# Weight-stationary matmuls of a hybrid encoder: the high and low parts of the tokens as one moving stream of 512 columns

## The chip, the cores and the metric

The kernel runs on one core of one Trainium2 chip. The metric is the device time of one execution in microseconds; for the kernel before it is the median of three runs.

## What is computed

The reference is an encoder of two layers over 256 positions of width 1024, in fp32. Each layer has three sub-layers behind an RMSNorm:

```python
for l in range(DEPTH):
    h = rmsnorm(x, mix_norm_g[l])
    x = x + hybrid_mixer(h, ...)      # h @ w_in, then attention, SSD and Fourier branches, gated and projected
    h = rmsnorm(x, xattn_norm_g[l])
    m = rmsnorm(mem, mem_norm_g[l])
    x = x + memory_cross_attention(h, m, ...)
    h = rmsnorm(x, ffn_norm_g[l])
    x = x + (silu(h @ w_gate) * (h @ w_up)) @ w_down
```

The SSD branch takes the columns x, B and C of `h @ w_in` (3072 columns) through a depthwise convolution of 7 taps along the positions, and then SiLU. The FFN is 2816 wide.

## The kernel before

Every large product is made of three fp32r matmuls: both factors are split into a part `hi` (rounded to fp32r) and a rest `lo`, and hi·hi + hi·lo + lo·hi is accumulated in PSUM. The weights arrive as a stream of 125 pieces per layer, 1 MB each (`PLAN`). `load_next` (L310) issues a piece's DMA on SyncE, `split_next` (L321) makes `wh` on ScalarE (L327) and `wl` on VectorE (L328). `done` (L342) splits the piece three after the one just used (NHL = 3 buffers of each kind), so a piece's `wl` is written while the pieces ahead of it are used.

Two helpers use the pieces. `lin` (L362) keeps tokens stationary and moves 512 weight columns per matmul (L357 to L359). `lina` (L401) keeps 128 weight columns stationary and moves the 256 tokens, so that its result stands transposed, channels on partitions; it serves the 12 pieces per layer of B, C and x (`xbc_pieces`, L1091) and 18 pieces of FFN gate and up (L1426). A `lina` piece is 8 contraction tiles by 256 columns; its two blocks of 128 columns share one PSUM bank, and each block runs, per contraction tile:

```python
T.matmul(o, hi[:, w0:w0 + P], sh[:, k, :], start=kt == 0, stop=False)
T.matmul(o, hi[:, w0:w0 + P], sl[:, k, :], start=False, stop=False)
T.matmul(o, lo[:, w0:w0 + P], sh[:, k, :], start=False, stop=kt == npk - 1)
```

The accumulators rotate over four banks (`acc`, L235); four others (`tp`) serve transposes and small products. When a piece of x, B or C is done, `conv_pair` (L696) copies the bank to SBUF on ScalarE (L699) and leaves the convolution (12 VectorE instructions, L710, and what is around them) as a background task. In the FFN `gate_f` applies SiLU straight from the bank (L1415) and `up_f` multiplies straight from the bank (L1419) before it splits the result for the down projection (L1422, L1423).

All other work (convolution, SSD, attention, Fourier, norms) is written as generators in seven lanes. `pump` (L281) runs them, piece by piece, against a budget of VectorE microseconds; a task that yields SOON or LATER is held back for some pumps (NWAIT = 1 for the norm lane, WAIT = 4). SBUF scratch comes in slots of 4 KB (23) and 2 KB (13) per partition: a foreground request that finds four or fewer free ones runs background steps until more are free (`slot`, L198, RESERVE = 4), and a background task waits until the slots that it declares are there. Within an engine the compiler's scheduler then orders the instructions, except on TensorE inside `ordered()`.

Below, piece n is the n-th of a layer, from 0; pieces 6 to 9 are B and C, 10 and 11, 24 and 25, 30 and 31, 38 and 39 are x, 14 to 17 gate columns, 95 and up the FFN's.

Of the kernel before, what the change touches and what calls it, by code (L numbers as in the profile page):

```python
# [31 lines left out]
NRAW, NHL = 3, 3  # L32
NS4, NS2 = 23, 13
LATER, SOON = "later", "soon"
LANES = ("n", "s", "c", "a", "t0", "t1", "f")
WAIT = 4
XWAIT = 3
NWAIT = 1
CAP = 6.0
# [136 lines left out]
def trunk(ctx: ExitStack, tc: tile.TileContext, a, out):  # L176
# [12 lines left out]
    def nm(p):  # L189
# [4 lines left out]
    slots = {4: deque(sp.ring(4096, name=f"r4_{i}") for i in range(NS4)),  # L194
             2: deque(sp.ring(2048, name=f"r2_{i}") for i in range(NS2))}
    owner = {}

    def slot(size, shape, dt):  # L198
        keep = 0 if running[0] else RESERVE
        while len(slots[size]) <= keep and step():  # L200
            pass
        if not slots[size]:
            raise RuntimeError(f"no slot of {size} KB")
        r = slots[size].popleft()
        t = r.tile(shape, dt, name=nm("s%d_" % size))
        owner[id(t)] = (size, r, t)
        return t
# [154 lines left out]
    def lin(act, npieces, on_done, nk=8, seg=None, us=BUDGET, par=False, before=None, mid=None):  # L362
# [5 lines left out]
        for si, n in enumerate(segs):  # L368
# [3 lines left out]
            for tt in range(2):  # L372
                if tt and not si and mid:
                    mid()
                for i, (w, k0, npk, n0, n_), (hi, lo) in ps:
                    if first is None:
                        first = n0
                    for c0 in range(0, n_, 512):
                        for kk in range(npk):
# [5 lines left out]
                            kt = k0 + kk  # L385
                            sh, sl = act(kt)
                            k = cnt[tt, ch]
# [13 lines left out]
    def lina(act, npieces, on_done, us=BUDGET):  # L401

        for _ in range(npieces):
            i, (w, k0, npk, n0, n_), (hi, lo) = take()
            us_ = us * npk * n_ / 2048
            for c0 in range(0, n_, 256):
                if c0:
                    pump(us_ / 2)
                nb = min(2, (n_ - c0) // P)
                ps = acc()  # L410
                with ordered():
                    for b in range(nb):
                        for kt in range(npk):
                            sh, sl = act(kt)
                            w0 = kt * n_ + c0 + b * P
                            o = ps[:, b * S:(b + 1) * S]
                            k = kt % 4
                            T.matmul(o, hi[:, w0:w0 + P], sh[:, k, :], start=kt == 0, stop=False)  # L418
                            T.matmul(o, hi[:, w0:w0 + P], sl[:, k, :], start=False, stop=False)  # L419
                            T.matmul(o, lo[:, w0:w0 + P], sh[:, k, :], start=False, stop=kt == npk - 1)  # L420
                on_done(n0 + c0, ps[:, :nb * S].rearrange("p (a b) -> p a b", a=nb))
            if n_ <= 256:
                pump(us_ / 2)
            done(i, us_)

# [60 lines left out]
    def put_f(pt, hl, tt, scale=None, n=4, par=False):  # L486

        hi, lo = hl
        pv = pt[:, :n * P].rearrange("p (a b) -> p a b", a=n)
        o = slice(tt, S, 2) if par else slice(tt * P, tt * P + P)  # L490
        if scale is None:
            A.copy(hi[:, :n, o], pv)  # L492
            V.tensor_sub(lo[:, :n, o], pv, hi[:, :n, o].bitcast(F32))  # L493
        else:
            A.activation(hi[:, :n, o], pv, AF.Copy, scale=scale)
            V.scalar_tensor_tensor(lo[:, :n, o], pv, scale, hi[:, :n, o].bitcast(F32),
                                   op0=ALU.mult, op1=ALU.subtract)

    def ftiles(n):
# [9 lines left out]
    nc.sync.dma_start(rb[32:35, :], a["c_sel"])  # L509
    h = ftiles(2)  # L510
    load_next()
# [184 lines left out]
    def conv_pair(ps, blk, cw, fin):  # L696

        u = s2([P, 2, S])
        A.copy(u, ps)  # L699

        def work():
# [3 lines left out]
            for b in range(2):  # L705
# [6 lines left out]
                yield 2.0  # L712
            free(u)
            A.activation(t, v, AF.Tanh, scale=0.5)
# [297 lines left out]
    for l in range(L):  # L1012
# [55 lines left out]
        def dt_columns():  # L1068
# [5 lines left out]
            for kt in range(8):  # L1074
                sh, sl = hb(kt)
# [41 lines left out]
        for n, tok in enumerate(ORDER):  # L1117
# [46 lines left out]
        free(h)  # L1164
        drain()
# [27 lines left out]
        gbx = bcast(a["xattn_norm_g"][l:l + 1, :], D)  # L1193
        hx = ftiles(2)

# [163 lines left out]
        lin(fl(hx), 4, query, seg=[1, 1, 1, 1])  # L1359
        free(hx)  # L1360
        vx.extend((s4([P, 2, 512], F32R), s4([P, 2, 512], F32R)) for _ in range(2))
# [19 lines left out]
        gbf = bcast(a["ffn_norm_g"][l:l + 1, :], D)  # L1381
        hf = ftiles(2)
        lin(fl(ox), 4, residual(gbf, hf), seg=[1, 3], before=drain)
# [42 lines left out]
        for c in range(9):  # L1426
            lina(fb, 1, gate_f)
            lina(fb, 1, up_f)
        free(hf)
        if l + 1 < L:  # L1430
            gbn = bcast(a["mix_norm_g"][l + 1:l + 2, :], D)
            h = ftiles(2)
            fin = residual(gbn, h)
# [46 lines left out]
```

## Time and profile before

| | |
|---|---|
| median of 3 runs | 1614.32 us (1613.74 to 1614.4) |
| the profiled execution | 1612.18 us, of it span 1610.1 us |
| TensorE matmuls | 8994, busy 99% of the span |
| VectorE busy | 1163.8 us (72%) |
| ScalarE busy | 956.5 us (59%) |
| GpSimd busy | 43.8 us (3%) |
| granted TensorE clock | 1.000 |

Busy matmul rows overlap, since a matmul starts before its predecessor's modelled end. So the cost of a matmul is read as the distance from one start to the next, and a wait of TensorE as idle time in front of an instruction.

### The profile page before, as it was taken

The page shows a single profiled execution, that of the slowest core. Times are in us where ns is not written, and L with a number is a line of the kernel's source. Part 1 is how long each engine was busy: PE and PEld are TensorE (multiplying, and loading weights), DVE is VectorE, ACT ScalarE, POOL GpSimd, SP SyncE. Part 2 cuts the span into 40 slices and gives each one's busy share as a digit, 9 for nine tenths or more (in the row PEclk, how much of TensorE's full clock was granted, in tenths as well). Part 3 has the DMA queues.
Part 4 walks back from the last instruction along what each step waited for, and adds up shares of the span by engine and source line. Part 5 has one row for each costly group of instructions (what it writes and reads, how often), then busy time and mean ns, then how long its engine had stood idle before and what let it go on. Part 6 is the DMA issues. An engine that isn't in the chain of part 4 may idle for free.

```text
span 1610.1 us, 22777 instructions
## 1 busy us (share of the span) xinstructions
PE 1592.1 (99%) x8994; PEld 1381.0 (86%) x8994; DVE 1163.8 (72%) x1777; ACT 956.5 (59%) x1587; POOL 43.8 (3%) x47
## 2 busy tenths in 40 slices
PE   8999999999999999999999999999999999999999
PEld 6998888888887888999889888888888878889997
DVE  5999997889757566555478999978886576565543
ACT  5666868787445664444356678677964457554442
POOL 0000000000000100000000000000100001000000
PEclk9999999999999999999999999999999999999999
DMA  8446655455556444555554577455555545345552
GB/s 298 159 161 230 223 182 181 167 196 192 196 196 223 177 153 162 198 183 184 183 190 146 182 230 242 154 189 179 172 185 203 202 181 196 131 169 175 183 190 95
DMA packets 84579, 299.46 MB, mean 186 GB/s; under 512 B 7305, under 2 KB 46857, under 8 KB 52728
## 3 DMA queue, kind: packets, MB, share of 16 engines
q1 hardware_dynamic: 84472, 298.01, 52.8%
q8 instruction: 70, 1.15, 0.3%
q14 instruction: 37, 0.30, 0.1%
HBM read 296.77 MB, written 1.22 MB: 185 GB/s over the span
## 4 chain that ended last, share of the span: by engine, by line
PE 91%; DVE 4%; ACT 2%; DMA 1%; POOL 1%; issue 1%; SPq 0%; DVEq 0%; ACTq 0%; POOLq 0%
PE acc L358 20%; PE acc L357 20%; PE acc L359 20%; PE acc L418 7%; PE acc L419 7%; PE acc L420 7%; PE tp L869 1%; PE tp L477 1%; PE tp L357 1%; PE tp L359 1%; PE tp L358 1%; PE tp L619 1%; DVE wl L328 1%; PE tp L940 1%; ACT wh L327 1%; PE tp L870 1%
## 5 line engine op out<-in xcount | busy, mean ns | idle before, releaser
L328 DVE TENSOR_TENSOR wl<-wr,wh 128x2048 fp32r<-128x2048 f32 (+1 forms) x256 | 572.6, 2239 | 278.5 <-ACT wh L327 277.9
L327 ACT CAST wh<-wr 128x2048 fp32r<-128x2048 f32 (+1 forms) x256 | 477.6, 1867 | 387.8 <-PE acc L359 184.3
L357 PE MATMUL acc<-wh,s 128*128 128x512 f32 x1520 | 604.4, 398 | 0.1
L358 PE MATMUL acc<-wl,s 128*128 128x512 f32 x1520 | 599.6, 395 | 1.6 <-DVE wl L328 1.6
L359 PE MATMUL acc<-wh,s 128*128 128x512 f32 x1520 | 596.2, 393 | 0.0
L358 PEld LDWEIGHTS acc<-wl,s 128*128 128x128 f32 x1520 | 288.0, 189 | 61.7 <-DVE wl L328 3.9
L357 PEld LDWEIGHTS acc<-wh,s 128*128 128x128 f32 x1520 | 287.9, 189 | 59.3 <-issue 1.4
L359 PEld LDWEIGHTS acc<-wh,s 128*128 128x128 f32 x1520 | 287.8, 189 | 58.0 <-issue 0.4
L418 PE MATMUL acc<-s,wh 128*128 128x256 f32 x960 | 273.3, 285 | 0.0
L419 PE MATMUL acc<-s,wh 128*128 128x256 f32 x960 | 271.7, 283 | 0.0
L420 PE MATMUL acc<-s,wl 128*128 128x256 f32 x960 | 271.6, 283 | 0.0
L418 PEld LDWEIGHTS acc<-s,wh 128*128 128x128 f32 x960 | 184.1, 192 | 1.1 <-issue 0.7
L419 PEld LDWEIGHTS acc<-s,wh 128*128 128x128 f32 x960 | 184.2, 192 | 0.8 <-issue 0.5
L420 PEld LDWEIGHTS acc<-s,wl 128*128 128x128 f32 x960 | 184.1, 192 | 0.0
L710 DVE SCALAR_TENSOR_TENSOR s<-s,cw,s 128x254 f32<-128x254 f32 (+2 forms) x288 | 120.9, 476 | 0.3
L841 ACT ACTIVATE s<-s,nacs 128x128 f32<-128x128 f32 x128 | 46.4, 392 | 13.4 <-DVE s L852 5.6
L844 ACT ACTIVATE s<-s,dt 128x128 f32<-128x128 f32 x128 | 45.3, 394 | 0.0
L842 DVE SCALAR_TENSOR_TENSOR s<-s,nacs,s 128x128 f32<-128x128 f32 x128 | 42.4, 344 | 3.5 <-ACT s L841 3.5
L845 DVE SCALAR_TENSOR_TENSOR s<-s,dt,s 128x128 f32<-128x128 f32 x128 | 41.5, 343 | 0.0
L493 DVE TENSOR_TENSOR s<-tp,s 128x512 fp32r<-128x512 f32 x56 | 36.9, 683 | 5.3 <-ACT s L492 5.2
L1199 DVE TENSOR_TENSOR X<-X,acc 128x512 f32<-128x512 f32 x24 | 16.4, 684 | 27.9 <-PE acc L359 27.9
L461 ACT ACTIVATE s<-X 128x512 f32<-128x512 f32 x24 | 15.1, 630 | 35.6 <-DVE X L1199 33.4
(224 smaller groups left out, 1418.8 us busy)
## 6 DMA issues: line engine op xcount, KB each, us to landing
wr<-in_wstream SPq DMA_DIRECT2D x248, 1024.0 KB, 4.8
s<-dd SPq DMA_DIRECT2D x32, 512.0 KB, 5.1
s<-in_wstream SPq DMA_DIRECT2D x6, 512.0 KB, 3.3
s<-vd SPq DMA_DIRECT2D x12, 256.0 KB, 5.9
wr<-in_wstream SPq DMA_DIRECT2D x8, 256.0 KB, 5.3
s<-in_ssd_norm_g SPq DMA_DIRECT2D x8, 256.0 KB, 3.2
s<-in_memT SPq DMA_DIRECT2D x4, 512.0 KB, 6.4
X<-in_x SPq DMA_DIRECT2D x2, 512.0 KB, 3.6
```

Source lines behind the costliest of these rows:

```text
L327: A.copy(hi[:, c], raw[:, c])
L328: V.tensor_sub(lo[:, c], raw[:, c], hi[:, c].bitcast(F32))
L357: T.matmul(o, sh, mh, start=start, stop=False)
L358: T.matmul(o, sh, ml, start=False, stop=False)
L359: T.matmul(o, sl, mh, start=False, stop=stop)
L418: T.matmul(o, hi[:, w0:w0 + P], sh[:, k, :], start=kt == 0, stop=False)
L419: T.matmul(o, hi[:, w0:w0 + P], sl[:, k, :], start=False, stop=False)
L420: T.matmul(o, lo[:, w0:w0 + P], sh[:, k, :], start=False, stop=kt == npk - 1)
L710: V.scalar_tensor_tensor(v[:, b, i0:i1], u[:, b, i0 + k - 3:i1 + k - 3], c[:, k:k + 1], v[:, b, i0:i1], op0=ALU.mult, op1=ALU.add)
L841: A.activation(E[:, j, :], b[:, 1, :], AF.Identity, bias=nacs[:, tt, 32 + hf:33 + hf])
L842: V.scalar_tensor_tensor(E[:, j, :], b[:, 0, :], nacs[:, tt, hf:hf + 1], E[:, j, :], op0=ALU.add, op1=ALU.min)
L844: A.activation(W[:, j, :], cbd[:, tt, 0, :], AF.Copy, scale=dt[:, tt, hf:hf + 1])
```

## The change

`lina` gives each block of 128 columns a PSUM bank of its own. The stationary `hi` weights are loaded once per contraction tile, and the tokens' `hi` and `lo` move as one stream of 2 x 256 columns, so that hi·hi lands in one half of the bank and hi·lo in the other. The `lo` weights still move the tokens' `hi` alone, into the first half. The two halves are added afterwards: on GpSimd after two copies in `conv_pair`, on VectorE from PSUM in the FFN (`halves`). For the two-part stream a norm's output (`h`, `hx`, `hf`) now has `hi` and `lo` in one tile, from two new 8 KB slots per pair, and the 4 KB slots fall from 23 to 19. NWAIT goes from 1 to 2, which holds back the transposes of a norm for one pump more.

```diff
-NS4, NS2 = 23, 13
+NS4, NS2, NS8 = 19, 13, 2
-NWAIT = 1
+NWAIT = 2
     def slot(size, shape, dt):
-        keep = 0 if running[0] else RESERVE
+        keep = 0 if running[0] or size == 8 else RESERVE
...
     def lina(act, npieces, on_done, us=BUDGET):
+            ps = []
+            for b in range(n_ // P):
+                ps.append(acc().rearrange("p (a b) -> p a b", a=2))
                 with ordered():
+                    for kt in range(npk):
+                        sh, _, hl = act(kt)
+                        k, w0, last = kt % 4, kt * n_ + b * P, kt == npk - 1
+                        small = lambda: T.matmul(ps[b][:, 0, :], lo[:, w0:w0 + P], sh[:, k, :], start=False, stop=False)
+                        if last:
+                            small()
+                        T.matmul(ps[b], hi[:, w0:w0 + P], hl[:, :, k, :], start=kt == 0, stop=last)
+                        if not last:
+                            small()
+            on_done(n0, ps)
...
+    def inputs_f():
+        ts = [slot(8, [P, 2, 4, S], F32R) for _ in range(2)]
+        return [(t[:, 0], t[:, 1], t) for t in ts]
...
     def conv_pair(ps, blk, cw, fin):
-        u = s2([P, 2, S])
-        A.copy(u, ps)
+        uu = s4([P, 2, 2, S])
+        for b in range(2):
+            A.copy(uu[:, b], ps[b])
+        u = uu[:, :, 0, :]
+        G.tensor_tensor(u, u, uu[:, :, 1, :], op=ALU.add)
...
+        def halves(t, ps):
+            for b in range(2):
+                A.copy(t[:, b], ps[b][:, 1, :])
+                V.tensor_add(t[:, b], t[:, b], ps[b][:, 0, :])
         def gate_f(n0, ps):
-            gs[n0] = s2([P, 2, S])
-            A.activation(gs[n0], ps, AF.Silu)
+            t = gs[n0] = s2([P, 2, S])
+            halves(t, ps)
+            A.activation(t, t, AF.Silu)
         def up_f(n0, ps):
-            t = gs[n0]
-            V.tensor_mul(t, t, ps)
+            t, r = gs[n0], s2([P, 2, S])
+            halves(r, ps)
+            V.tensor_mul(t, t, r)
```

The order of TensorE in an FFN gate piece, before (`s_618`, `s_619` are the tokens' `hi` and `lo`, `acc_117` the bank):

```order
L418 MATMUL acc_117<-s_618_5455,wh_5759 128x256
L419 MATMUL acc_117<-s_619_5456,wh_5759 128x256
L420 MATMUL acc_117<-s_618_5455,wl_5760 128x256
L418 MATMUL acc_117<-s_618_5455,wh_5759 128x256
L419 MATMUL acc_117<-s_619_5456,wh_5759 128x256
```

and in the changed kernel, at the end of a block and the start of the next (`s_614`, `s_615` hold both parts of the first and the last four contraction tiles):

```order
L419 MATMUL acc_114<-s_615_5318,wh_5969 128x512
L416 MATMUL acc_114<-s_615_5318,wl_5970 128x256 x2
L419 MATMUL acc_114<-s_615_5318,wh_5969 128x512
L419 MATMUL acc_115<-s_614_5317,wh_5969 128x512
L416 MATMUL acc_115<-s_614_5317,wl_5970 128x256
```

Two matmuls of 512 and 256 columns stand where three of 256 stood, and the next block goes to another bank.

The order of VectorE in the mixer of the first layer, between the `wl` of piece 16 and that of piece 17, before (L710 is the convolution, L786 the split of a finished pair of B or C):

```order
L328 TENSOR_TENSOR wl_1212<-wr_1033,wh_1211 128x2048
L786 TENSOR_TENSOR s_80_584<-s_145_1167,s_79_583 128x512
L710 SCALAR_TENSOR_TENSOR s_159_1287<-s_118_935,cw_209,s_159_1287 128x254
L710 SCALAR_TENSOR_TENSOR s_168_1372<-s_127_1020,cw_209,s_168_1372 128x254
L710 SCALAR_TENSOR_TENSOR s_159_1287<-s_118_935,cw_209,s_159_1287 128x253
L710 SCALAR_TENSOR_TENSOR s_168_1372<-s_127_1020,cw_209,s_168_1372 128x255
L710 SCALAR_TENSOR_TENSOR s_168_1372<-s_127_1020,cw_209,s_168_1372 128x253
L328 TENSOR_TENSOR wl_1246<-wr_1132,wh_1245 128x2048
```

and in the changed kernel the last ten rows ahead of the same `wl` (lines 12 higher there: L722 was L710, L826 was L814, the masking of C·B, L329 was L328):

```order
L722 SCALAR_TENSOR_TENSOR s_157_1243<-s_137_1065,cw_205,s_157_1243 128x255
L826 SCALAR_TENSOR_TENSOR s_159_1261<-tp_110,tri 128x128
L722 SCALAR_TENSOR_TENSOR s_157_1243<-s_137_1065,cw_205,s_157_1243 128x255
L826 SCALAR_TENSOR_TENSOR s_159_1261<-tp_110,tri 128x128
L722 SCALAR_TENSOR_TENSOR s_157_1243<-s_137_1065,cw_205,s_157_1243 128x254
L826 SCALAR_TENSOR_TENSOR s_159_1261<-tp_110,tri 128x128
L722 SCALAR_TENSOR_TENSOR s_157_1243<-s_137_1065,cw_205,s_157_1243 128x253
L826 SCALAR_TENSOR_TENSOR s_159_1261<-tp_110,tri 128x128
L722 SCALAR_TENSOR_TENSOR s_157_1243<-s_137_1065,cw_205,s_157_1243 128x253
L329 TENSOR_TENSOR wl_1305<-wr_1073,wh_1304 128x2048
```

Between the two `wl` stand 6 instructions before and 42 in the changed kernel: 22 of L722, 16 of L826, 2 of L727 and 2 of L798. On TensorE the 24 small matmuls of C·B (L357 to L359 into `tp`), which stood at pieces 17 and 18, now stand at pieces 14 to 16.

## Rows read from the trace of the kernel before

**Rows 1.** The page: busy time, VectorE in 40 slices, chain that ended last.
```profile
PE 1592.1 (99%) x8994; PEld 1381.0 (86%) x8994; DVE 1163.8 (72%) x1777; ACT 956.5 (59%) x1587; POOL 43.8 (3%) x47
...
DVE  5999997889757566555478999978886576565543
...
PE 91%; DVE 4%; ACT 2%; DMA 1%; POOL 1%; issue 1%; SPq 0%; DVEq 0%; ACTq 0%; POOLq 0%
```

**Rows 2.** Groups by line: `lina`'s first matmul; count | busy us, mean ns | idle before.
```profile
L418 PE MATMUL acc<-s,wh 128*128 128x256 f32 x960 | 273.3, 285 | 0.0
```

**Rows 3.** Timeline, TensorE in an FFN piece: start us, length us, engine, line, operation.
```profile
660.11 0.28 PE L418 MATMUL acc<-s,wh 128*128 128x256 f32 x1
660.23 0.28 PE L419 MATMUL acc<-s,wh 128*128 128x256 f32 x1
...
660.47 0.28 PE L418 MATMUL acc<-s,wh 128*128 128x256 f32 x1
```

**Rows 4.** Timeline, TensorE in a piece of `lin`, down projection.
```profile
754.93 0.39 PE L357 MATMUL acc<-wh,s 128*128 128x512 f32 x1
...
755.61 0.39 PE L357 MATMUL acc<-wh,s 128*128 128x512 f32 x1
```

**Rows 5.** Timeline, TensorE, Fourier branch: moving operand in four runs of 66 columns.
```profile
68.44 0.29 PE L357 MATMUL tp<-s,s 128*128 128x264 f32 x1
68.57 0.29 PE L358 MATMUL tp<-s,s 128*128 128x264 f32 x1
```

**Rows 6.** Groups by line and shape: the cast to `wh`; reads of PSUM.
```profile
L327 ACT CAST wh<-wr 128x2048 fp32r<-128x2048 f32 x248 | 473.1, 1907 | 387.5 <-PE acc L359 184.3 <-issue 149.0 <-PE acc L419 42.2
...
L699 ACT COPY s<-acc 128x512 f32<-128x512 f32 x24 | 13.8, 575 | 0.0
...
L796 ACT ACTIVATE s<-tp 128x256 f32<-128x256 f32 x32 | 10.7, 381 | 4.9 <-PE tp L795 4.7
...
L1249 DVE SCALAR_TENSOR_TENSOR s<-tp,gk,s 128x256 fp32r<-128x256 f32 x16 | 7.5, 479 | 0.5 <-ACT s L1248 0.4
```

**Rows 7.** Stretches of 10 us: length, then busy us and count by engine.
```profile
60.00:70.00 10.00, 10.00 (x85) 10.00 (x84) 9.61 (x23) 5.71 (x6) 0.00 (x0) 1.00 0.49 170
...
120.00:130.00 10.00, 10.00 (x46) 8.29 (x45) 10.00 (x16) 5.27 (x5) 0.00 (x0) 1.00 0.53 202
```

**Rows 8.** Timeline: `wl` of pieces 16 and 17, first `lo` matmul of piece 17.
```profile
111.28 2.29 DVE L328 TENSOR_TENSOR wl<-wr,wh 128x2048 fp32r<-128x2048 f32 x1 [0.24 <-ACT wh L327]
...
116.23 2.29 DVE L328 TENSOR_TENSOR wl<-wr,wh 128x2048 fp32r<-128x2048 f32 x1
...
125.20 0.39 PE L358 MATMUL acc<-wl,s 128*128 128x512 f32 x1
```

**Rows 9.** Groups by line: the VectorE work that now stands ahead of piece 17.
```profile
L710 DVE SCALAR_TENSOR_TENSOR s<-s,cw,s 128x254 f32<-128x254 f32 (+2 forms) x288 | 120.9, 476 | 0.3
...
L814 DVE SCALAR_TENSOR_TENSOR s<-tp,tri 128x128 f32<-128x128 f32 x32 | 7.6, 284 | 0.8 <-ACT s L816 0.3 <-PE tp L359 0.3
```

**Rows 10.** Timeline: two waits of TensorE late in the first layer's mixer.
```profile
351.81 0.33 PE L907 MATMUL tp<-idn,s 128*128 128x128 f32 x1 [0.70 <-DVE s L674]
...
382.71 0.50 PE L358 MATMUL acc<-wl,s 128*128 128x512 f32 x1 [0.80 <-DVE wl L328]
```

**Rows 11.** Timeline: GpSimd alone, beside VectorE; then a GpSimd group by line.
```profile
404.52 0.70 POOL L450 TENSOR_TENSOR gst<-gst,half_c 128x2 f32<-128x2 f32 x1 [41.38 <-DVE gst L449]
...
415.85 1.12 POOL L450 TENSOR_TENSOR gst<-gst,half_c 128x2 f32<-128x2 f32 x1 [10.63 <-DVE gst L449]
...
415.73 0.69 DVE L1063 TENSOR_TENSOR s<-s,s 128x512 f32<-128x512 f32 x1
...
L450 POOL TENSOR_TENSOR ars<-ast,half_c 128x16 f32<-128x16 f32 x6 | 18.2, 3035 | 478.8 <-DVE ast L449 478.8
```

**Rows 12.** A norm's transposes: timeline of one, and the group of all.
```profile
615.79 0.44 PE L477 MATMUL tp<-idn,s 128*128 128x128 f32 x2 [0.39 <-DVE s L469]
...
L477 PE MATMUL tp<-idn,s 128*128 128x128 f32 x96 | 15.6, 292 | 2.4 <-DVE s L469 2.3
```

More of the change, by code (lines that the diff above doesn't have):

```diff
@@ L194, in trunk @@
     slots = {4: deque(sp.ring(4096, name=f"r4_{i}") for i in range(NS4)),
-             2: deque(sp.ring(2048, name=f"r2_{i}") for i in range(NS2))}
+             2: deque(sp.ring(2048, name=f"r2_{i}") for i in range(NS2)),
+             8: deque(sp.ring(8192, name=f"r8_{i}") for i in range(NS8))}
     owner = {}
     def slot(size, shape, dt):
-        keep = 0 if running[0] else RESERVE
+        keep = 0 if running[0] or size == 8 else RESERVE
         while len(slots[size]) <= keep and step():
@@ L385, in lin @@
                             kt = k0 + kk
-                            sh, sl = act(kt)
+                            sh, sl = act(kt)[:2]
                             k = cnt[tt, ch]
@@ L404, in lina @@
             i, (w, k0, npk, n0, n_), (hi, lo) = take()
[L405 to L410, printed above, removed]
-                with ordered():
[L412 to L421, printed above, removed]
+            ps = []
+            for b in range(n_ // P):
+                if b and b % 2 == 0:
+                    pump(us / 4)
+                ps.append(acc().rearrange("p (a b) -> p a b", a=2))
+                with ordered():
+                    for kt in range(npk):
[8 more added lines that the diff above has]
+            on_done(n0, ps)
             if n_ <= 256:
-                pump(us_ / 2)
-            done(i, us_)
+                pump(us / 2)
+            done(i, us)
     def fl(tiles):
@@ L486, in put_f @@
     def put_f(pt, hl, tt, scale=None, n=4, par=False):
-        hi, lo = hl
+        hi, lo = hl[:2]
         pv = pt[:, :n * P].rearrange("p (a b) -> p a b", a=n)
@@ L497, in put_f, with free_f @@
                                    op0=ALU.mult, op1=ALU.subtract)
+    def inputs_f():
+        ts = [slot(8, [P, 2, 4, S], F32R) for _ in range(2)]
+        return [(t[:, 0], t[:, 1], t) for t in ts]
+    def free_f(h):
+        free(*(t for _, _, t in h))
     def ftiles(n):
@@ L509, in trunk @@
     nc.sync.dma_start(rb[32:35, :], a["c_sel"])
-    h = ftiles(2)
+    h = inputs_f()
     load_next()
@@ L712, in work @@
                 yield 2.0
-            free(u)
+            free(uu)
             A.activation(t, v, AF.Tanh, scale=0.5)
@@ L1074, in dt_columns @@
             for kt in range(8):
-                sh, sl = hb(kt)
+                sh, sl = hb(kt)[:2]
                 k = kt % 4
@@ L1163, in trunk @@
                 free(R["oT"], ga)
-        free(h)
+        free_f(h)
         drain()
@@ L1193, in trunk @@
         gbx = bcast(a["xattn_norm_g"][l:l + 1, :], D)
-        hx = ftiles(2)
+        hx = inputs_f()
         def residual(gb, dst, last=False):
@@ L1359, in trunk @@
         lin(fl(hx), 4, query, seg=[1, 1, 1, 1])
-        free(hx)
+        free_f(hx)
         vx.extend((s4([P, 2, 512], F32R), s4([P, 2, 512], F32R)) for _ in range(2))
@@ L1381, in trunk @@
         gbf = bcast(a["ffn_norm_g"][l:l + 1, :], D)
-        hf = ftiles(2)
+        hf = inputs_f()
         lin(fl(ox), 4, residual(gbf, hf), seg=[1, 3], before=drain)
@@ L1411, in trunk @@
         lin(fb, 2, up_0)
+        def halves(t, ps):
+            for b in range(2):
+                A.copy(t[:, b], ps[b][:, 1, :])
+                V.tensor_add(t[:, b], t[:, b], ps[b][:, 0, :])
         def gate_f(n0, ps):
-            gs[n0] = s2([P, 2, S])
-            A.activation(gs[n0], ps, AF.Silu)
+            t = gs[n0] = s2([P, 2, S])
+            halves(t, ps)
+            A.activation(t, t, AF.Silu)
         def up_f(n0, ps):
-            t = gs[n0]
-            V.tensor_mul(t, t, ps)
+            t, r = gs[n0], s2([P, 2, S])
+            halves(r, ps)
+            V.tensor_mul(t, t, r)
+            free(r)
             c = n0 // P
@@ L1428, in trunk @@
             lina(fb, 1, up_f)
-        free(hf)
+        free_f(hf)
         if l + 1 < L:
             gbn = bcast(a["mix_norm_g"][l + 1:l + 2, :], D)
-            h = ftiles(2)
+            h = inputs_f()
             fin = residual(gbn, h)
```

## The prediction, made before the changed kernel ran

> **What bounds the kernel now.** I read the page first, then the groups by line, then timelines of the places that the change touches. The page [rows 1] shows TensorE busy for 99% of the span and 91% of the chain that ended last on TensorE; VectorE is busy for 72% on average but for nine tenths or more in slices 2 to 6 and again around slice 22, the first part of each layer's mixer. So time is won where TensorE has less to stream, and lost where it comes to wait for VectorE.
>
> Since matmul rows overlap, I take distances between starts. In a FFN piece of `lina` the starts are 0.12 us apart, three matmuls of 256 columns taking 0.36 us per contraction tile [rows 3]. In `lin` three matmuls of 512 columns take 0.68 us, 0.227 each [rows 4]. From 256 to 512 columns a matmul grows by 0.107 us, so 256 columns cost 0.107 and each matmul pays another 0.013 that does not depend on its width. The idle time before the `lina` matmuls is 0.0 [rows 2]: they run back to back.
>
> **The change part by part.** *Fewer matmuls.* A contraction tile's 0.360 us become 0.227 + 0.120 = 0.347, so 13.3 ns less (each figure rounded to a few ns). There are 960 tiles (60 pieces of 16) [rows 2]: **960 x 13.3 ns = 12.8 us**, 7.7 in the FFN and 5.1 in the mixer. TensorE is the bound there, so this lies on the path. Two things could spoil it. The moving operand now has two runs of 256 columns; nearest is the Fourier product with runs of 66, where 264 columns start 0.13 us apart [rows 5], against 0.123 by the law above. I take no penalty, with 7 ns x 960 = 6.7 us as the bad end and nothing below zero. And a weight load must hide beside 256 columns, but all 2880 already do that.
>
> The Trainium skill's page "TensorE: Matmul & The Clock Gate", section "Back-to-back issue gap", gives a warm gap of the columns over 2.4 GHz plus 2.5 ns. By that a saved matmul is worth 2.5 ns and the term 2.4 us instead of 12.8; the rows show 120 and 227 ns where it would have 109 and 216, so I keep the rows.
>
> *More to evict.* In the convolution 24 ScalarE copies of 512 columns come on top, 0.575 us each [rows 6]: 13.8 us. In the FFN 72 ScalarE copies of 256 columns (0.38, the row of L796) and 72 VectorE additions (0.48, the row of L1249) come on top: 27 and 35 us. A gate and an up piece give TensorE 11.1 us; in that time VectorE then has two splits (2.3 each) [rows 8], four additions, one multiplication and one split of the result (0.69 each, as L1063) [rows 11], 7.9 us, and ScalarE two casts of 1.9, four copies, SiLU and a cast of 512 columns (0.6 each, as L699), 6.5 us. Both fit. A piece now takes two of the four banks, so a bank has to be empty 5.5 us after its piece's end rather than three pieces later; a cast in front (1.9), two copies and two additions make 3.6. I cost it at nothing; without that cover TensorE would wait for a bank in each of 36 pieces.
>
> *Additions on GpSimd.* The kernel before has no GpSimd row of this shape. Nearest are GpSimd's 0.70 us for a power of two columns and VectorE's 0.69 for a sum of 512 [rows 11]; together I take 1.4 us, between VectorE's 0.69 and the 3.0 that GpSimd needs for a power of 16 columns [rows 11]. The 24 of them are no work of a busy engine (GpSimd 3%) [rows 1], and the convolution reads their results a piece later. But the second line there shows GpSimd at 1.12 us where it needs 0.70 alone: it began while VectorE ran an addition of two SBUF operands (the third line) and ended 0.55 after that one's end. So one engine can hold up the other, and a held VectorE is not free. I take 0.5 us of TensorE time per layer, between nothing and the rival's price below.
>
> *VectorE's order in the mixer.* `uu` now takes 4 KB slots where there were 2 KB ones, and a foreground request that finds few runs background work at once. The order shows the effect: 42 VectorE instructions between the `wl` of pieces 16 and 17, where 6 stood. Of these, 22 convolution steps at 120.9/288 = 0.42 make 9.2 us and 16 maskings at 0.24 make 3.8; four more of 512 columns at 0.62 (0.69 less the overlap of neighbours) make 2.5: 15.5 us [rows 9, 11]. Before, the `wl` of piece 16 ended at 113.5, that of piece 17 at 118.5, and TensorE asked for it at 125.2 [rows 8], a lead of 6.7 us. VectorE is full from 60 to 130 us (9.6 and 10.0 of 10 in the first and last of seven stretches) [rows 7], so it can't start the surplus sooner. Now the `wl` of piece 17 ends near 113.5 - 1 + 15.5 + 2.2 = 130. TensorE asks at 125.2 - 1.3 (six `lina` pieces at 0.21 each) + 2.9 (24 small matmuls at 0.12 moved ahead) + 0.4 (four transposes) = 127. I take **2 us of wait per layer**; bounds are 0 and 8, if GpSimd's six additions by then hold VectorE too. Two more such clusters stand ahead of pieces 37 (34 instructions) and 45 (50). Before, clusters stood ahead of pieces 39 (40), 47 (30) and 53 (74), and only the last made TensorE wait: 0.80 and, just before, 0.70 [rows 10]. I take 0.5 for the two new and give back 1.5 for the old. Net **+1.0 per layer, +2.0**.
>
> SyncE's queue gets no new DMAs; the requests that SSD makes for its decay rows come two to eight pieces later, with the tasks, and stay behind weights that are in good time.
>
> *Cross-attention.* With four 4 KB slots fewer after `hx` is free, the last attention transposes (L1332) move 8 matmuls, 1.8 us, ahead. I take a wait of 0.5 per layer, of 0 to 1.8: +1.0.
>
> *Norms later.* At three of six norms the first transposes move back by 12 matmuls (2.7 us), which covers a wait of 0.39 us as in [rows 12]; the second ones of three move ahead by one to three matmuls, 0.2 to 0.7 us each. All norm transposes together idle TensorE for 2.4 us, so the gain lies between 2.4 and about -1; I take -0.6 us.
>
> The sum is -12.8 + 2.0 + 1.0 (GpSimd) + 1.0 - 0.6 = **-9.4 us**. The profiled execution took 1612.18 (1610.1 of span, the rest around it), so 1602.8 for such a one; it stood 2.1 us under the median of 1614.32, so **1605** against that median.
>
> **The rivals.** *The clusters cost nothing*: no new wait, the old ones gone (3.0 us in two layers), norms at their best. Then -12.8 - 3.0 - 2.4 = -18.2, about 1596. For it: the page's idle time is small everywhere, and three clusters cost 1.5 us per layer before [rows 10]. Against it: the one at piece 17 stands where VectorE is full. Chance 0.25.
>
> *VectorE becomes the bound of the mixer*, the case on the other side. GpSimd's 12 additions per layer hold it for 1.4 us each, 16.8 us per layer, in a stretch that has a spare of about 1.5 us in 70 [rows 7]; the wait then shows at piece 17 and at the transposes that follow convolutions. With nine of the 16.8 and the 2 us on TensorE's path it is 22 us for two layers, 1614.3 - 13.4 + 22 = 1623. It decides from 6.7 us of new waits per layer on; below that the kernel is still faster. For it speak [rows 7, 11]. Against it: [rows 11] show only GpSimd waiting, and TensorE has a lead of some 6.7 us over `wl` to use up. The Trainium skill, "SBUF — State Buffer", section "Who interferes with whom", says that a VectorE instruction with two SBUF inputs and a GpSimd instruction that reads SBUF lock each other out, whichever comes second; [rows 11] agree for one direction, and no row here shows the other. Chance 0.1.
>
> *The matmuls don't get cheaper*, since the two-run stream pays or the width-independent part comes back: -6 or less, then +3.4 of waits, 1611 to 1617. [Rows 3 to 5] speak against it. Chance 0.1.
>
> **How the numbers follow.** The forecast, matmuls as priced and small waits, has 0.55 and reaches from 1600 to 1611. The range 1597 to 1613 takes in most of the first rival and part of the third, and leaves out about 2 in 10. A measurement can tell 0.2% or 3.2 us from no change. Faster than 1611.1: all of the first rival, nearly all of the forecast, 0.80. Within: the third rival's larger part and an edge of the forecast, 0.11. Slower than 1617.5: the second rival, 0.09.
>
> **What would show it.** Right, if in an FFN piece the profile has starts 0.227 and 0.12 us apart in turn, a gate and up pair takes 11.1 us instead of 11.5, and the groups show no idle time before them; if the wait at the first `lo` matmul of piece 17 is a few us, ended by VectorE's `wl`; if GpSimd's additions last near 1.4 us. Wrong, if `lina`'s matmuls wait for banks, if their distance is over 0.235, if waits of TensorE on VectorE in the mixers add up to more than 13 us, or if neither VectorE rows nor waits grow there at all.

## The result, and the profile after

The changed kernel takes 1621.46 us (median of 5 runs, 1621.21 to 1622.71), the kernel before, on the same chip in the same minutes, 1614.0 (5 runs): a ratio of 1.0052, 95% interval 1.0041 to 1.0063. It is slower by 7 to 8 us where 9.4 less were forecast, and lies outside the range. One execution of e3 below, of 3589 us, is left out of its times.

The changed kernel's page, to be read against [rows 1]: its span, busy times, and VectorE and GpSimd in 40 slices.

```profile
span 1620.9 us, 21018 instructions
...
PE 1588.3 (98%) x8034; PEld 1331.2 (82%) x8034; DVE 1213.1 (75%) x1849; ACT 989.9 (61%) x1683; POOL 83.0 (5%) x71
...
DVE  5999897988957665666479997969888576666653
...
POOL 0110010100000100000001001110100001000000
```

There are 960 matmuls fewer, but TensorE's matmuls are busy for only 3.8 us less. VectorE has 49.3 us more, though the additions in the FFN (`halves`, L1428) account for 30.1 of them; 19 us have come to work that did not change. Where they went stands in the groups by line, which answer to [rows 2, 9]:

```profile
L419 PE MATMUL acc<-s,wh 128*128 128x512 f32 x960 | 334.7, 399 | 0.0
...
L722 DVE SCALAR_TENSOR_TENSOR s<-s,cw,s 128x253 f32<-128x253 f32 (+2 forms) x288 | 135.9, 525 | 0.1
...
L711 POOL TENSOR_TENSOR s<-s 128x512 f32<-128x512 f32 x24 | 39.6, 1648 | 354.3 <-ACT s L709 354.3
L1428 DVE TENSOR_TENSOR s<-s,acc 128x256 f32<-128x256 f32 x72 | 30.1, 418 | 33.5 <-ACT s L1427 33.5
```

`lina`'s matmuls still wait for nothing (0.0), so no bank is late there. A step of the convolution, the same instruction as before, takes 525 ns instead of 476 [rows 9], 15.0 us in all; GpSimd's 24 additions take 1.65 us each.

The waits of TensorE in the first layer's mixer (30 to 520 us): what waited for what, us in total, times, longest.

```profile
PE acc L359 <- DVE wl L329: 2.5, 1, 2.5
PE tp L359 <- DVE s L959: 1.6, 1, 1.6
PE tp L807 <- DVE s L727: 1.3, 1, 1.3
PE tp L358 <- ACT s L958: 1.0, 1, 1.0
PE tp L358 <- ACT s L797: 0.7, 1, 0.7
PE tp L616 <- DVE s L884: 0.6, 1, 0.6
```

They sum to 7.7 us; the same view of the second layer (832 to 1322 us) has 2.2, 1.9, 1.3, 0.6 and 0.6, 6.6 us. Before, each layer had the two waits of [rows 10], 1.5 us, and both are gone. So 14.3 us stand where 3.0 stood: **+11.3**. The first row is the forecast wait at piece 17. The others, Fourier (L958, L959), the transposes behind a convolution (L807) and the B and C products (L797), were not forecast.

After the longest wait something follows that no row of before had. First TensorE's timeline from the wait at piece 17 on; then stretches of the changed kernel: length, then busy us and count of TensorE, its weight loads, VectorE, ScalarE and GpSimd, the granted clock, DMA share, GB/s.

```profile
136.57 0.50 PE L359 MATMUL acc<-wl,s 128*128 128x512 f32 x1 [2.55 <-DVE wl L329]
...
138.50 0.63 PE L359 MATMUL acc<-wl,s 128*128 128x512 f32 x1
138.93 0.63 PE L360 MATMUL acc<-wh,s 128*128 128x512 f32 x1
...
141.47 0.40 PE L359 MATMUL acc<-wl,s 128*128 128x512 f32 x1
141.71 0.39 PE L360 MATMUL acc<-wh,s 128*128 128x512 f32 x1
```

```profile
137.50:140.90 3.40, 3.40 (x10) 2.62 (x9) 3.40 (x5) 2.32 (x6) 0.00 (x0) 0.50 0.84 311
140.90:150.00 9.10, 9.10 (x41) 7.51 (x41) 8.33 (x12) 5.96 (x10) 0.00 (x0) 1.00 0.87 293
```

TensorE had waited for 2.55 us until 136.57. From 137.5 to 140.9 the granted clock is 0.50, the 1.2 GHz level, and the matmuls of 512 columns start 0.43 us apart; at 1.00, behind it, they start 0.23 to 0.24 apart. So nearly half of the 3.4 us, 1.6, is lost, and the second layer has the same stretch behind its 2.2 us: **+3.2**.

Last, the norms. Waits of TensorE from 500 to 1600 us, before and then in the changed kernel:

```profile
PE tp L477 <- DVE s L469: 2.3, 6, 0.5
```

```profile
PE acc L360 <- DVE s L494: 3.1, 3, 1.2
...
PE tp L478 <- DVE s L470: 0.8, 2, 0.4
```

The transposes wait less, but at three norms the next matmul now waits for the `lo` part that is split from them: **+1.6**. TensorE's first wait, ahead of all that changed, differs too, before and then in the changed kernel:

```profile
PE tp L525 <- ACT s L518: 7.8, 1, 7.8
```

```profile
PE tp L534 <- ACT s L527: 9.5, 1, 9.5
```

These 1.8 us (7.78 and 9.55) can't be put down to the change: e4 below, which has the change, waits for 7.8 there. With them and the matmuls' -7.4 (below) the sum is -7.4 + 11.3 + 3.2 + 1.6 + 1.8 = 10.5; the spans of the two profiled executions (1612.18 and 1622.71 us) differ by 1620.9 - 1610.1 = 10.8, more than the medians, which are 7.5 apart.

### The profile page after: what moved, and what is told of

It is laid out like the page before. It is cut to its first block, busy times and chain, and to the rows that moved or that the text cites. A ratio compares the mean times of both kernels' runs of the same rounds, so it can differ in the third digit from the quotient of the medians.

```text
span 1620.9 us, 21018 instructions
## 1 busy us (share of the span) xinstructions
PE 1588.3 (98%) x8034; PEld 1331.2 (82%) x8034; DVE 1213.1 (75%) x1849; ACT 989.9 (61%) x1683; POOL 83.0 (5%) x71
## 5 line engine op out<-in xcount | busy, mean ns | idle before, releaser
L329 DVE TENSOR_TENSOR wl<-wr,wh 128x2048 fp32r<-128x2048 f32 (+1 forms) x256 | 572.9, 2240 | 229.1 <-ACT wh L328 228.5
L328 ACT CAST wh<-wr 128x2048 fp32r<-128x2048 f32 (+1 forms) x256 | 478.2, 1870 | 241.8 <-PE acc L360 206.4
L359 PE MATMUL acc<-wl,s 128*128 128x512 f32 x1520 | 599.9, 395 | 4.9 <-DVE wl L329 4.8
L359 PEld LDWEIGHTS acc<-wl,s 128*128 128x128 f32 x1520 | 288.8, 190 | 64.4 <-DVE wl L329 6.3
L419 PE MATMUL acc<-s,wh 128*128 128x512 f32 x960 | 334.7, 399 | 0.0
L416 PE MATMUL acc<-s,wl 128*128 128x256 f32 x960 | 249.9, 281 | 0.0
L419 PEld LDWEIGHTS acc<-s,wh 128*128 128x128 f32 x960 | 173.8, 188 | 33.5 <-issue 0.7
L416 PEld LDWEIGHTS acc<-s,wl 128*128 128x128 f32 x960 | 181.2, 189 | 10.8 <-issue 0.5
L722 DVE SCALAR_TENSOR_TENSOR s<-s,cw,s 128x253 f32<-128x253 f32 (+2 forms) x288 | 135.9, 525 | 0.1
L1427 ACT COPY s<-acc 128x256 f32<-128x256 f32 x72 | 26.8, 372 | 93.6 <-PE acc L419 89.8
L711 POOL TENSOR_TENSOR s<-s 128x512 f32<-128x512 f32 x24 | 39.6, 1648 | 354.3 <-ACT s L709 354.3
L1428 DVE TENSOR_TENSOR s<-s,acc 128x256 f32<-128x256 f32 x72 | 30.1, 418 | 33.5 <-ACT s L1427 33.5
L709 ACT COPY s<-acc 128x512 f32<-128x512 f32 x48 | 27.7, 581 | 27.1 <-PE acc L419 27.1
L494 DVE TENSOR_TENSOR s<-tp,s 128x512 fp32r<-128x512 f32 x56 | 36.8, 687 | 6.1 <-ACT s L493 6.1
```

Of the source, the lines that this page charges most:

```text
L328: A.copy(hi[:, c], raw[:, c])
L329: V.tensor_sub(lo[:, c], raw[:, c], hi[:, c].bitcast(F32))
L359: T.matmul(o, sh, ml, start=False, stop=False)
L416: small = lambda: T.matmul(ps[b][:, 0, :], lo[:, w0:w0 + P], sh[:, k, :], start=False, stop=False)
L419: T.matmul(ps[b], hi[:, w0:w0 + P], hl[:, :, k, :], start=kt == 0, stop=last)
L722: V.scalar_tensor_tensor(v[:, b, i0:i1], u[:, b, i0 + k - 3:i1 + k - 3], c[:, k:k + 1], v[:, b, i0:i1], op0=ALU.mult, op1=ALU.add)
```

## The experiments

Ratios are to the kernel before, run beside each kernel on the same chip (1613.5 to 1613.9 us); times are medians.

### The changed kernel with one part taken back

**e1, two slots of 2 KB.** The cluster ahead of piece 17 comes from the 4 KB slot; this edit takes it away and leaves GpSimd's additions, two of 256 columns for each one of 512.

```diff
-        uu = s4([P, 2, 2, S])
+        uu = [s2([P, 2, S]) for _ in range(2)]
...
-        G.tensor_tensor(u, u, uu[:, :, 1, :], op=ALU.add)
+        for b in range(2):
+            G.tensor_tensor(uu[b][:, 0, :], uu[b][:, 0, :], uu[b][:, 1, :], op=ALU.add)
```

> The changed kernel with the two copies of conv_pair in two 2 KB slots instead of one 4 KB slot (the GpSimd addition becomes two of 256 columns, the matmuls stay). No cluster is left ahead of pieces 17 and 45; the clusters stand ahead of 39, 47 and 53 again. Slot theory (the 4 KB request runs background work early and puts 42 VectorE instructions ahead of piece 17): the wait of 2.55 us at piece 17 and those on L958, L959, L797 and L727 go, 1621.5 falls by 8 to 12 us, to about 1611. GpSimd theory (VectorE is held by the additions, wherever they stand): VectorE's busy time stays about 19 us above what the added instructions explain, waits turn up elsewhere in the mixer, and the time stays above 1617.

Measured: 1621.22 us, ratio 1.0047 (1.0032 to 1.0062). The wait at piece 17 is gone and the time has not changed. The waits up to 520 us are now elsewhere:

```profile
PE tp L590 <- DVE s L582: 2.8, 1, 2.8
PE acc L358 <- ACT s L496: 2.7, 1, 2.7
PE tp L358 <- ACT s L958: 1.9, 1, 1.9
PE tp L807 <- DVE s L727: 1.4, 1, 1.4
```

The second row (at 510.6 us) stands behind the mixer and behind a load of `memT` that took 7.8 us to land (5.7 in the kernel before); the second layer has none like it. The first row, with 3.4 us at half clock behind it in each layer, is no cost of GpSimd's: e13 has the same wait without GpSimd. It comes with the two 2 KB slots, so e1 takes one wait away and brings another, and does not price the cluster.

**e2, the addition on VectorE.** The 4 KB slot and its cluster stay, GpSimd goes.

```diff
-        G.tensor_tensor(u, u, uu[:, :, 1, :], op=ALU.add)
+        V.tensor_tensor(u, u, uu[:, :, 1, :], op=ALU.add)
```

> The changed kernel with the addition of conv_pair on VectorE instead of GpSimd, slots as in the change; the cluster ahead of piece 17 has 52 instructions. GpSimd theory: the convolution steps fall from 525 ns to 476, VectorE is free of some 19 us and pays 24 x 0.69 = 16.5 us of additions, so nearly even: 1619 to 1622. Slot theory: the longer cluster makes the wait at piece 17 longer, 3 to 6 us instead of 2.5, so 1621 to 1626.

Measured: 1621.27 us, ratio 1.0045 (1.0028 to 1.0062). Waits of the first mixer:

```profile
PE acc L359 <- DVE wl L329: 3.9, 1, 3.9
PE tp L807 <- DVE s L727: 2.9, 2, 2.1
```

The convolution's steps are back at 479 ns and the Fourier waits are gone, so GpSimd's hold is real; but the wait at piece 17 has grown (3.9 us, and 5.3 in the second layer), and a stretch of 6.8 us at half clock begins inside it in each layer. Neither e1 nor e2 alone tells what costs.

**e3, the norms not later** (NWAIT = 1).

> The changed kernel with NWAIT back at 1. Norm theory (a norm held one pump longer is late for the first matmul that reads it): the three waits of about 1.0 us in front of L360 on VectorE's L494 go, three of about 0.4 in front of the transposes come back, net 1.5 to 3 us faster, 1619. Rival (the prediction's): the later transposes gain 0.6 us, so it gets 0 to 1 us slower, 1622.

Measured: 1618.6 to 1623.7 us, ratio 1.0044 (1.0027 to 1.0061). The waits at L494 are gone, those at the transposes are back with 2.0 us, and the change in time can't be told from none.

**e4, the two parts as one run** of 512 columns.

```diff
-        ts = [slot(8, [P, 2, 4, S], F32R) for _ in range(2)]
+        ts = [slot(8, [P, 4, 2, S], F32R) for _ in range(2)]
...
```

> The changed kernel with the tokens' hi and lo of a contraction tile next to each other in the 8 KB tile, so that the moving operand is one run of 512 columns. Order and waits as in the change. Run theory (two runs 4 KB apart cost 6 to 8 ns per matmul): the distance behind L419 falls from 235 ns to 227 and its sum with L416 from 353 to 347, 960 x 6 ns = 6 us faster, 1615.5. Rival (the alternation of widths or the weight loads cost it): 353 stays, no change, 1621.5.

Measured: 1622.54 us, ratio 1.0053 (1.0038 to 1.0068); the distances are unchanged (0.235 us behind L419 and 0.118 behind L416 in both). So two runs are not what keeps a contraction tile at 0.353 us.

### The change's halves by themselves

**e5, the new stream in the FFN alone.** The mixer keeps the old `lina`, as `lina1`, and the old `conv_pair`; NWAIT is 1, as before.

```diff
-            lina(hb, 2, f)
+            lina1(hb, 2, f)
...
```

> The new stream in the FFN alone; the mixer's pieces, its convolution and NWAIT = 1 as in the kernel before, the slots as in the changed one. Theory (VectorE of the mixer has no room for the change, the FFN has): TensorE's waits in the mixer are those of before, and the FFN keeps its 2.2 us per layer, so 1614 less 4.5, 1608 to 1611. Rival (the smaller pool of 4 KB slots, or the evictions of the FFN, cost as much): 1613 or more.

Measured: 1609.28 us, ratio 0.9972 (0.9961 to 0.9982), as the theory had it.

**e6, the new stream in the mixer alone.** `gate_f` and `up_f` are the old ones; NWAIT is 1.

```diff
-            lina(fb, 1, gate_f)
-            lina(fb, 1, up_f)
+            lina1(fb, 1, gate_f)
+            lina1(fb, 1, up_f)
...
```

> The new stream in the mixer alone, the FFN's gate and up pieces as before, NWAIT = 1. Theory: the mixer's waits and the stretch at half clock behind them stand as in the changed kernel, so 1621 plus the 4.5 us that the FFN no longer saves, 1624 to 1627. Rival (the loss lies in the FFN or in what follows it): 1614 to 1618.

Measured: 1625.0 us, ratio 1.0073 (1.0059 to 1.0086). So the whole loss lies in the mixer, and the FFN gains (e5).

**e7, as e5, with equal widths side by side.** A block runs four matmuls of 512, eight of 256, four of 512.

```diff
+                    for kt in range(npk // 2):
+                        move(kt, True)
+                    for kt in range(npk):
+                        move(kt, False)
+                    for kt in range(npk // 2, npk):
+                        move(kt, True)
```

> As e5, but in each block four matmuls of 512, then the eight of 256, then the other four of 512, where the two widths alternate. Theory (a change of width costs the 3 ns per matmul that were not forecast): distances of 227 and 120 ns inside the runs, 0.347 us per contraction tile, another 576 x 6 ns = 3.5 us less than e5. Rival (a 512 matmul over 128 stationary columns costs 235 ns wherever it stands): distances as in e5, the same time within 1 us.

Measured: 1607.83 us, ratio 0.9965 (0.9952 to 0.9979). Timelines of an FFN piece, first the changed kernel's, then that of e7 (where L417 has 512 columns and L419 has 256):

```profile
666.12 0.40 PE L419 MATMUL acc<-s,wh 128*128 128x512 f32 x1
666.36 0.28 PE L416 MATMUL acc<-s,wl 128*128 128x256 f32 x1
...
667.18 0.40 PE L419 MATMUL acc<-s,wh 128*128 128x512 f32 x1
```

```profile
685.43 2.00 PE L417 MATMUL acc<-s,wh 128*128 128x512 f32 x8
687.27 1.12 PE L419 MATMUL acc<-s,wl 128*128 128x256 f32 x8
688.23 2.00 PE L417 MATMUL acc<-s,wh 128*128 128x512 f32 x8
```

Alternating, three tiles take 1.06 us, 0.353 each. Grouped, eight of 512 take 1.84 and eight of 256 take 0.96: 0.230 + 0.120 = 0.350 a tile. Half of the missing 6 ns was the change of width: 576 x 3 ns = 1.7 us, and the time fell by 1.5, hardly more than two such medians scatter. The expectation of 0.347 and 3.5 us was too high.

**e8, the kernel before with NWAIT = 2 alone.**

> The kernel before with NWAIT = 2 alone. Theory (a late transposition moves the wait from the transposes to the next matmul): the same within 1 us, idle time at the transposes smaller and as much new before the matmul that reads their result. Rival (it gains what was forecast): 0.6 to 2.4 us less.

Measured: 1614.67 us, ratio 1.0006 (0.9997 to 1.0015). Waits from 500 to 1600 us, against the 2.3 us above:

```profile
PE acc L359 <- DVE s L493: 2.9, 3, 1.0
PE tp L477 <- DVE s L469: 0.8, 2, 0.4
```

The wait moves from the transposes to the matmul that reads them and grows by 1.4 us; in the time it can't be told from nothing.

### Slots and GpSimd, each alone

Both start from e7, whose mixer is that of the kernel before.

**e9, the slots alone.** It has the changed kernel's clusters (42 instructions ahead of the `wl` of piece 17) and nothing else of its mixer.

```diff
-        u = s2([P, 2, S])
+        uu = s4([P, 2, 2, S])
+        u = uu[:, :, 0, :]
...
```

> e7 (old matmuls in the mixer, 1607.8) with one edit: the convolution's input takes a 4 KB slot, as in the changed kernel; no second copy, no addition. VectorE then has the changed kernel's clusters, 42 instructions ahead of the wl of piece 17. Theory of the clusters (they alone make the waits of the mixer): a wait of 2 us or more at piece 17 of each layer with half clock behind it, 1613 to 1618. Rival (VectorE only lacks room because of GpSimd and the evictions): 1607 to 1610, the wait at piece 17 under 1 us.

Measured: 1606.76 us, ratio 0.9957 (0.9944 to 0.9969). The cluster makes TensorE wait, but less, and no half clock follows. The wait in the timeline of TensorE (it is the only wait of 0.5 us or more in that mixer), and the stretch behind it:

```profile
132.60 0.50 PE L359 MATMUL acc<-wl,s 128*128 128x512 f32 x1 [1.39 <-DVE wl L329]
```

```profile
133.00:145.00 12.00, 12.00 (x55) 9.91 (x54) 11.90 (x16) 10.48 (x23) 0.00 (x0) 1.00 0.77 270
```

The old waits of [rows 10], 1.5 us, are gone in exchange. The wait fits neither expectation (2 us or more, under 1 us), the time lies just below the rival's: the clusters alone cost nothing.

**e10, GpSimd alone.** One copy and one slot as before; ScalarE halves while it copies and GpSimd doubles.

```diff
-        A.copy(u, ps)
+        A.activation(u, ps, AF.Identity, scale=0.5)
+        G.tensor_tensor(u, u, u, op=ALU.add)
```

> e7 with one edit: GpSimd doubles the convolution's input, which ScalarE has halved while copying it (24 additions of 512 columns, nothing else). VectorE's order is that of e7. Theory of GpSimd (it holds VectorE by 0.8 us for each addition and the fourier and convolution transposes wait behind): convolution steps of about 525 ns instead of 476 and 1612 to 1618. Rival (VectorE's lead covers it): 1607.5 to 1610.

Measured: 1623.28 us, ratio 1.006 (1.0047 to 1.0074): 24 additions on an otherwise idle engine cost 15.5 us against e7, more than expected. VectorE and TensorE run the same instructions in the same order in both. The groups of the convolution in e7; of the additions, the convolution and the ScalarE step ahead of it in e10; and of that step in the changed kernel:

```profile
L748 DVE SCALAR_TENSOR_TENSOR s<-s,cw,s 128x254 f32<-128x254 f32 (+2 forms) x288 | 121.0, 476 | 0.3
```

```profile
L738 POOL TENSOR_TENSOR s<-s 128x512 f32<-128x512 f32 x24 | 58.7, 2448 | 374.9 <-ACT s L737 312.7 <-DVE dpp L785 49.8 <-issue 6.8
...
L749 DVE SCALAR_TENSOR_TENSOR s<-s,cw,s 128x254 f32<-128x254 f32 (+2 forms) x288 | 127.3, 497 | 10.8 <-ACT s L746 10.4
...
L746 ACT ACTIVATE s<-s,cw 128x256 f32<-128x256 f32 x48 | 27.0, 596 | 33.9 <-POOL s L738 30.6 <-DVE s L1014 3.3
```

```profile
L719 ACT ACTIVATE s<-s,cw 128x256 f32<-128x256 f32 x48 | 26.6, 602 | 3.6 <-POOL s L711 3.6
```

The cost came by two ways, not by one. The steps are held (6.3 us), less than expected; and GpSimd is held too, 2.45 us an addition, so that ScalarE stands idle for 30.6 us in front of the step that reads the sum (L746), and VectorE for 10.8 us in front of the convolution. TensorE waits for what stands behind, 6.5 us in the first mixer at seven places, and 3.4 us at half clock follow in each layer. The largest of these waits, and the one on `wl`:

```profile
PE tp L657 <- ACT s L646: 1.9, 1, 1.9
PE tp L834 <- DVE s L911: 1.3, 1, 1.3
...
PE acc L359 <- DVE wl L329: 0.8, 1, 0.8
```

The wait on `wl` is that of before; the new ones stand at matmuls that ask for other results of VectorE and ScalarE. And the 15.5 us are not the price of the additions in the changed kernel: there the same ScalarE step waits for GpSimd for 3.6 us (the last of the groups above). e10 shows both ways, and not what each costs.

### VectorE's additions, with and without the clusters

**e11, the mixer from PSUM.** The new stream in the mixer too, grouped as in e7, NWAIT = 1; the halves are added as in the FFN.

```diff
...
-        uu = s4([P, 2, 2, S])
-        for b in range(2):
-            A.copy(uu[:, b], ps[b])
-        u = uu[:, :, 0, :]
-        G.tensor_tensor(u, u, uu[:, :, 1, :], op=ALU.add)
+        u = s2([P, 2, S])
+        for b in range(2):
+            A.copy(u[:, b], ps[b][:, 1, :])
+            V.tensor_add(u[:, b], u[:, b], ps[b][:, 0, :])
```

> The new stream in the mixer too, in the order of e7, NWAIT = 1, but each half is copied by ScalarE and the other added to it by VectorE from PSUM into a 2 KB slot, as in the FFN: no GpSimd, no 4 KB slot, no cluster at piece 17; 48 VectorE additions of about 0.48 us, 23 us in all, and 384 tiles cheaper by 10 ns, 3.8 us. Theory (the mixer's VectorE has no room, whoever holds it): waits remain, 1610 to 1618. Rival (only GpSimd and the clusters cost): 1604 to 1606.

Measured: **1604.09 us**, ratio 0.9941 (0.9929 to 0.9954), the fastest of all and better than both kernels. It gains 3.7 us on e7, what its expectation had for the 384 tiles (3.8). The 48 additions are there, and the waits of TensorE in the mixer are again those of [rows 10], 0.8 and 0.7 us a layer:

```profile
L725 DVE SCALAR_TENSOR_TENSOR s<-s,cw,s 128x253 f32<-128x253 f32 (+2 forms) x288 | 128.3, 478 | 0.5
...
L714 DVE TENSOR_TENSOR s<-s,acc 128x256 f32<-128x256 f32 x48 | 19.2, 415 | 1.4 <-ACT s L713 1.4
```

VectorE carries 19.2 us more, about as much as GpSimd had held it for, and it costs nothing. So "VectorE has no room" is too simple: it has the lead of [rows 8] to use up.

**e12, e7 with one run.** The edit of e4 on e7.

> e7 with hi and lo of a contraction tile side by side, so that the 512 columns are one run. In e7 the 512-wide matmuls stand 231 ns apart where those of lin stand 227. Theory (two runs cost 4 ns, hidden in e4 by the alternation): 227, 576 x 4 ns = 2.3 us less than e7. Rival (something else makes the 4 ns): 231 and the same time within 1 us.

Measured: 1607.5 us, ratio 0.996 (0.9948 to 0.9973); the 512-wide matmuls stay 230 ns apart, so the two runs cost nothing. Why they are not at 227 as in `lin` stays open.

**e13, e11 with the addition in SBUF.** Two copies of 512 columns into two 2 KB slots, no cluster at piece 17.

```diff
...
+            A.copy(uu[b], ps[b])
...
+            V.tensor_tensor(uu[b][:, 0, :], uu[b][:, 0, :], uu[b][:, 1, :], op=ALU.add)
```

> e11 with the other form of addition: two ScalarE copies of 512 columns into two 2 KB slots and a VectorE addition of two SBUF halves in each; no cluster at piece 17. Theory (clusters and additions cost only together): near e11, 1602 to 1608, TensorE's waits in the mixer under 1 us each. Rival (this form of addition is what costs in e2): 1612 to 1622.

Measured: 1607.39 us, ratio 0.9962 (0.9949 to 0.9976), inside the theory's range. One thing missed it: the wait of 2.8 us at L594, which e1 has too (there L590), stands in each layer. So the addition in SBUF on VectorE, slots included, costs 3.3 us more than that from PSUM.

**e14, e11 with a 4 KB slot**, which puts the clusters back.

```diff
-        u = s2([P, 2, S])
+        uu = s4([P, 2, 2, S])
+        u = uu[:, :, 0, :]
...
```

> e11 with the result in a 4 KB slot, which puts the clusters back: 50 instructions ahead of the wl of piece 17, of them 42 as in e9 and the additions. Theory (only together): e9 had a wait of 1.4 us there with no lead left, and 12 additions of 0.42 us now stand ahead of it, so 4 to 7 us of wait at piece 17 of each layer with half clock behind it, 1612 to 1620. Rival (the form of the addition costs in e2): 1603 to 1607.

Measured: 1616.22 us, ratio 1.0016 (1.0008 to 1.0025), 12.1 us more than e11 by nothing but where the result lies and the order that follows from it; each engine runs the same instructions. This is what the theory expected. The wait at piece 17, and the stretch behind it:

```profile
136.76 0.80 PE L359 MATMUL acc<-wl,s 128*128 128x512 f32 x1 [4.94 <-DVE wl L329]
```

```profile
137.50:140.80 3.30, 3.30 (x10) 2.53 (x9) 3.30 (x5) 3.30 (x10) 0.00 (x0) 0.50 0.93 315
```

The second layer waits for 5.5 us there, and in both the half clock lasts 6.8 us and begins inside the wait. So the cluster costs nothing alone (e9), additions on VectorE cost nothing alone (e11, against a gain), and together they cost 12 us: the 6.7 us of lead hold one of the two. e2 has both as well, and its waits at piece 17 are like these.

## Why the prediction was wrong

**The step that failed is GpSimd's term, "0.5 us of TensorE time per layer", and the argument that kept it small, "TensorE has a lead of some 6.7 us over `wl` to use up".** The runs show three things in its place. First, "are no work of a busy engine" was an error: GpSimd was idle, but VectorE spent 19 us more on work that did not change, 15.0 of them on the convolution. Second, the lead had already been spent in the sum, on the cluster: e9, e11 and e14 show that it covers the cluster or the additions, and not both. Loads on the same stretch of one engine were costed one by one, each against the whole lead. Third, the lead over `wl` covers only the matmuls that read `wl`. In e10 no cluster uses the lead up at piece 17 and the wait on `wl` stays at 0.8, yet the kernel loses 15.5 us, by waits at transposes and products that ask for other results. In the changed kernel the Fourier waits (L958, L959) are of this kind: 4.5 us in two layers, absent in e2 and e9. "The convolution reads their results a piece later" did not hold everywhere either, as ScalarE's wait for GpSimd shows.

How the loss divides between GpSimd and the cluster stays open: e1 and e2 take one away each, but e1 brings a wait of its own and e2 puts the additions on VectorE behind the cluster, and e10 makes ScalarE wait far longer than the changed kernel does.

From -9.4 to the 10.8 by which the two executions differ, 20.2 us are missing. New waits make 8.3 of them (11.3 where the sum had 2.0 and 1.0), the matmuls 5.4, the half clock 3.2, the norms 2.2 and TensorE's first wait 1.8; cross-attention gives back 1.0. That leaves 0.3.

**The second rival** named the mechanism ("GpSimd's 12 additions per layer hold it") at a chance of 0.1, and its 1623 is near, in part by luck. It took VectorE to be held for 16.8 us per layer, and 9.6 were measured. Its own mark for a slower kernel, 6.7 us of new waits per layer, was not reached (6.2 and 5.1); the kernel is slower because the matmuls gave less and the half clock came on top, and it had neither. The prediction's sign of being wrong, more than 13 us of waits on VectorE in the mixers, did not show either: 10.1 of the 14.3 us are put down to VectorE, 4.2 to ScalarE.

One place in the changed kernel shows the lock in both directions, where [rows 11] had it in one. VectorE and GpSimd at 91 to 96 us:

```profile
91.34 2.28 DVE L329 TENSOR_TENSOR wl<-wr,wh 128x2048 fp32r<-128x2048 f32 x1
...
93.54 0.68 DVE L959 TENSOR_TENSOR s<-s,s 128x512 fp32r<-128x512 f32 x1
94.14 1.50 DVE L722 SCALAR_TENSOR_TENSOR s<-s,cw,s 128x253 f32<-128x253 f32 x1
```

```profile
64.14 1.36 POOL L711 TENSOR_TENSOR s<-s 128x512 f32<-128x512 f32 x1 [47.24 <-ACT s L709]
...
92.63 2.73 POOL L711 TENSOR_TENSOR s<-s 128x512 f32<-128x512 f32 x1 [3.74 <-ACT s L709]
```

GpSimd begins inside the `wl` and stays until 95.36, for 2.73 us where 1.36 were enough at 64.14; the convolution step that starts at 94.14 needs 0.48 us elsewhere and takes 1.50, ending at 95.64. The Trainium skill's page "SBUF — State Buffer", section "Who interferes with whom", has this lock between a VectorE instruction with two SBUF inputs and a GpSimd instruction that reads SBUF, whichever is second; with these rows the trace agrees for both. The prediction weighed that rule and priced it by the direction that it had seen.

**VectorE's order.** The wait at piece 17 was forecast at 2 us and is 2.55 and 2.23, and the old waits went as forecast. Its working gave 130 against 127, which is 3 and not 2, with a "- 1" that it does not explain. e9, with the cluster alone, waits for 1.4; but there the old matmuls bring TensorE to piece 17 later (an estimate: 6 pieces of 16 tiles at 0.362 instead of 0.354 us, 0.8 us), so most of the wait may well be the cluster's, as forecast. The waits forecast at pieces 37 and 45 did not come; those at Fourier, the convolution's transposes and the B and C products were not forecast. Net +2.0 was forecast for the clusters and +1.0 for GpSimd; measured are +11.3 of waits.

**The half clock was no term at all.** It is +3.2 us here: the two waits at piece 17 cost about 1.6 us more each than their length. When it comes stays open: the wait of 2.2 us at piece 17 of the second layer is followed by it here and not in e3 and e6.

**Fewer matmuls: the mechanism right, the size off.** Sums of start distances over the 960 tiles give 347.4 us before and 340.0 now, -7.4 instead of -12.8: 0.362 and 0.354 us a tile, where 0.360 and 0.347 were forecast. "Two things could spoil it" named two runs and the weight load; e4 and e12 rule the runs out, e7 shows that half of the missing 6 ns is the alternation of widths, which the law taken from long rows of one width could not show; where the other half comes from, the weight load included, stays open. The third rival, "-6 or less", was not it, though the distance behind a matmul of 512 columns, 0.235, lies at the edge of its sign: the gain is 7.4, and e5 and e7 are faster.

**Norms later** was -0.6 and is +1.6 by the waits, within what a run can tell (e3, e8): the term priced the transposes, and not the matmul that reads their `lo` part. **Cross-attention** was +1.0; no new wait stands there. **Evictions in the FFN** at nothing were right: TensorE's matmuls of `lina` wait for nothing, ScalarE's copies take 0.37 us and VectorE's additions 0.42, and e5 keeps the FFN's gain.

## What to carry to other kernels

Before work is put on an idle engine, ask whether its operands hold up the busy one: an addition of two SBUF operands on GpSimd was VectorE time here, while the same additions on VectorE itself were covered with one operand in PSUM (e11) and nearly so with both in SBUF (e13). A lead of an engine over its consumer is one budget for a stretch: add up all that the change puts on that stretch, late order and new work, and compare the sum once. It covers only the consumer for which it was read; the other matmuls that ask for that engine's results have leads of their own. And when a wait is taken away and the time stays (e1, e2), try each load alone on a kernel without the others (e9, e10, e11) and then together (e14), and see in the profile whether the edit brought a wait of its own (e1, e10).

## What had not been expected of the hardware

Matmuls of 512 and 256 columns in turn took 0.353 us a pair where runs of one width took 0.350 (0.230 and 0.120); in `lin` 512 columns take 0.227. Waits of TensorE of some 2 us and more were in most places followed by 3.4 or 6.8 us at 1.2 GHz (granted 0.50; a matmul of 512 columns every 0.43 us instead of 0.23), although TensorE was busy again for all or part of them; a wait of 1.4 us (e9) was not, nor was one of the two 2.8 us waits of e13. And a result's move from a 2 KB to a 4 KB slot, which changes no instruction but the order, cost 12.1 us (e14 against e11).
